# Filler matmuls placed behind the last scans' steps, and half of the attention's output projection moved into them

## The chip, the cores and the metric

The kernel runs on one core of one Trainium2 chip. The metric is device microseconds of one execution, of which the median over the runs is given. TensorE is called PE in the profile, VectorE DVE, ScalarE ACT, GpSimd POOL; SP is the engine that only issues DMAs here.

## The reference

One step of a decoder layer is computed for 1024 prompt tokens and for 8 samples of one token each, 1032 tokens in all, with a model width of 1024, all in float32:

```
h  = RMSNorm(x) * (1 + scale1) + shift1
z  = h @ w_in            # DeltaNet q|k|v, its gate, beta, decay; attention q, k, v; two branch gates ga, gb
y_a = GatedRMSNorm(GatedDeltaRule(conv4(q,k,v))) @ w_gdn_out      # 8 heads of 128
y_b = SlidingWindowSinkAttention(q, k, v) @ w_swa_out             # 16 query heads of 64, 4 kv heads, window 128
x  = x + gate1 * ((sigmoid(ga) * y_a + sigmoid(gb) * y_b) @ w_o)
h2 = RMSNorm(x) * (1 + scale2) + shift2
x  = x + gate2 * ((silu(dwconv3(h2 @ w_ffn_gate)) * (h2 @ w_ffn_up)) @ w_ffn_down)
y  = RMSNorm(x)
```

The prompt's gated delta rule runs in chunks from a zero state: per chunk a triangular inverse, and a recurrence over the chunks that carries a 128x128 state. The samples take one step of the same rule from states that are inputs (8 heads x 8 samples x 128x128), and give the new states back.

## The kernel before

**A product.** Every float32 product of the large projections is three matmuls on split operands: `mm3` (L168 to L170) multiplies high by high, high by low and low by high. An operand is split on ACT (L126, the high part) and DVE (L127, the rest). The split activations `h` (tiles b1h and b1l) stay resident in three parts of 384, 384 and 264 tokens (`PARTS`). A weight column of 128 outputs is one 512 KB load (L132), one split, and then, for each part, 8 blocks of 128 inputs with 3 matmuls each.

**The order.** The code is written as generators. `weave` runs several side by side, each with a priority and an increment, `later` runs a piece at a lower priority, and the scheduler of the framework then orders each engine's instructions from the priorities and its own estimate of the durations. What comes out is a fixed list for each engine, and each engine works its list from top to bottom: a matmul whose operand is late holds up all that stand behind it on PE. DMAs are issued from SP's list, a few from POOL's.

**The stages** that matter here, with their place in the profiled span:

- *Attention* (to 430 us): four groups of four query heads, each over 8 blocks of 128 tokens (`attention_block`): scores (L561, L562), transposes of the exponentials (L178), products with the values (L598, L600). Query and key projections lie between the blocks; none is left for the last ones.
- *Eight DeltaNet heads* (430 to 1182 us). For head h `weave` runs the triangular inverse (`unit_inverse`, L959 to L995, which goes through DRAM between its steps: `ud`, `MR`, `T`), the projections of head h+2, the gate projection of head h (`delta_gate`), the preparation of head h+1 (`delta_prepare`), and the scan (`delta_scan`). The scan has 8 chunks; a chunk is a chain of three steps on PE, each waiting for DVE or ACT: `rc<-S,K` (L870), `rc<-y,W` (L873), `rc<-s,kd` (L877), with two products for the output beside them (L880, L881).
- *Filler.* `gates()` is a generator of 16 tiles of work (8 for each branch gate): a column of `w_in`, 3 parts, 72 matmuls each, then tanh on ACT, a scaling on POOL and a store to DRAM (sgb, sga). `pieces(n)` pulls n x 8 of its steps. Each head pulls one tile at priority 10000, head 7 pulls the other eight within its `head_projections`.
- `turn_rows` in head 6 turns the input `x` in 9 chunks (load L771, 8 transposes, store L777) for later use; `last_rows` in head 7 gives back the last rows before the convolution (transposes of `zl`, copies L1027 to one of two `th` buffers, stores).
- *Branches* (1182 us on, `branches`). All of the attention's output `ob` is loaded and split in three parts (b2h, b2l), then y_b is computed: 8 columns of `w_swa_out` x 3 parts; the result times the gate is kept in SBUF (tiles t0 to t2, L1220). `sample_delta`, the samples' rule, is a generator that is stepped between these products: the loads of the states (b1h, b1l), small matmuls (L1084), 8 POOL products (L1124), 64 updates on DVE (L1126), 8 stores. Then y_a with `w_gdn_out`, then `w_o` and the second half, which the change leaves as it is.

## Time and profile before

| what | value |
|---|---|
| median of 3 runs | 2211.08 us (2209.51 to 2211.73) |
| profiled execution, its own time | 2216.06 us |
| span of the profiled execution | 2214.3 us |
| mean granted TensorE clock | 0.970 |
| PE busy / DVE / ACT / POOL | 96% / 60% / 36% / 14% of the span |

PE is busy nearly all of the time, so the table alone shows little. The stretches in which it isn't, and those in which the clock granted to it falls below full, are short and are found with busy times by stage. In the rows, "idle before, releaser" is time in which the engine had nothing to run, and what ended it.

### The profile page before, as it was taken

How to read it: one execution, taken by the hardware profiler on the slowest of the kernel's cores; microseconds unless marked ns; L12 is line 12 of the kernel's file. 1: busy time of each engine (PE TensorE's matmuls, PEld its weight loads, DVE VectorE, ACT ScalarE, POOL GpSimd, SP SyncE). 2: the span in 40 equal slices, each digit the busy share in tenths (PEclk: the TensorE clock that was granted, in tenths of full speed). 3: DMA queues.
4: the chain of work that ended last, by engine and by line, in shares of the span. 5: the costliest groups of instructions: out<-in, count | busy, mean ns of one | idle time of the engine just before them, and what ended most of it. 6: DMA issues, size and time to landing. Idle time of an engine off the chain costs nothing.

```text
span 2214.3 us, 41267 instructions
## 1 busy us (share of the span) xinstructions
PE 2123.2 (96%) x16573; PEld 1995.0 (90%) x16573; DVE 1335.3 (60%) x2892; ACT 801.2 (36%) x2037; POOL 303.3 (14%) x395
## 2 busy tenths in 40 slices
PE   7998999899899999999978999999999999999998
PEld 3695788699899999999968899999999999999998
DVE  4556667574474664755423565468776776866565
ACT  3445445433333334234332032344343433421102
POOL 2000000022122121121110200002332332100000
PEclk8998999799999999999988999999999999999999
DMA  9411333232232231232753663612323222253202
GB/s 340 140 40 39 115 117 106 82 79 49 73 83 69 53 91 52 65 89 73 199 140 107 206 187 99 184 61 68 108 70 96 68 94 70 96 215 129 88 3 78
DMA packets 271346, 228.16 MB, mean 103 GB/s; under 512 B 57566, under 2 KB 237697, under 8 KB 271138
## 3 DMA queue, kind: packets, MB, share of 16 engines
q1 hardware_dynamic: 269826, 221.23, 32.5%
q10 hardware_dynamic: 1152, 3.70, 0.4%
q8 instruction: 130, 2.13, 0.4%
q14 instruction: 62, 0.51, 0.1%
q0 software_dynamic: 176, 0.59, 0.1%
HBM read 175.51 MB, written 52.35 MB: 103 GB/s over the span
## 4 chain that ended last, share of the span: by engine, by line
PE 84%; DVE 6%; DMA 5%; ACT 2%; issue 1%; SPq 1%; POOL 0%; DVEq 0%; POOLq 0%; ACTq 0%
PE mm L168 19%; PE mm L169 18%; PE mm L170 18%; PE wv L168 2%; PE wv L169 2%; PE wv L170 2%; PE wy L170 2%; PE wy L168 2%; PE wy L169 2%; PE pv L600 1%; PE mm L252 1%; PE pv L598 1%; PE pt L178 1%; PE tp L178 1%; PE sc L561 1%
## 5 line engine op out<-in xcount | busy, mean ns | idle before, releaser
L168 PE MATMUL mm<-b1h,wh 128*128 128x384 f32 (+1 forms) x1440 | 476.0, 332 | 9.6 <-DVE kx L496 4.5
L170 PE MATMUL mm<-b1h,wl 128*128 128x384 f32 (+1 forms) x1440 | 469.2, 327 | 3.9 <-DVE wl L127 3.9
L169 PE MATMUL mm<-b1l,wh 128*128 128x384 f32 (+1 forms) x1440 | 468.8, 326 | 0.1
L168 PEld LDWEIGHTS mm<-b1h,wh 128*128 128x128 f32 x1440 | 274.3, 191 | 22.1 <-issue 6.3
L169 PEld LDWEIGHTS mm<-b1l,wh 128*128 128x128 f32 x1440 | 274.6, 191 | 8.6 <-issue 7.0
L170 PEld LDWEIGHTS mm<-b1h,wl 128*128 128x128 f32 x1440 | 274.0, 190 | 6.6 <-DVE wl L127 4.7
L126 ACT ACTIVATE wh<-raw 128x1024 fp32r<-128x1024 f32 x77 | 80.7, 1048 | 156.4 <-PE mm L169 103.0
L168 PE MATMUL mm<-b2h,wh 128*128 128x384 f32 (+1 forms) x384 | 123.9, 324 | 1.6 <-DVE t L1220 1.0
L168 PE MATMUL mm<-pk,w 128*128 128x260 f32 (+1 forms) x440 | 124.4, 283 | 0.9 <-ACT pk L126 0.6
L169 PE MATMUL mm<-pk,w 128*128 128x260 f32 (+1 forms) x440 | 124.2, 282 | 0.8 <-DVE pk L127 0.8
L169 PE MATMUL mm<-b2l,wh 128*128 128x384 f32 (+1 forms) x384 | 123.5, 322 | 1.2 <-DVE b2l L127 1.2
L170 PE MATMUL mm<-pk,w 128*128 128x260 f32 (+1 forms) x440 | 124.2, 282 | 0.0
L170 PE MATMUL mm<-b2h,wl 128*128 128x384 f32 (+1 forms) x384 | 122.7, 321 | 0.0
L127 DVE TENSOR_TENSOR wl<-raw,wh 128x1024 fp32r<-128x1024 f32 x76 | 93.7, 1233 | 45.6 <-ACT wh L126 44.7
L170 PE MATMUL mm<-bmh,pk 128*128 128x256 f32 (+1 forms) x380 | 108.6, 286 | 0.8 <-DVE pk L127 0.8
L168 PE MATMUL mm<-bmh,pk 128*128 128x260 f32 (+1 forms) x380 | 108.7, 286 | 0.0
L1342 DVE SCALAR_TENSOR_TENSOR x<-mm,mT,x 128x256 f32<-128x256 f32 (+2 forms) x133 | 63.4, 481 | 72.7 <-PE mm L170 70.3
L169 PE MATMUL mm<-bml,pk 128*128 128x260 f32 (+1 forms) x353 | 100.6, 285 | 0.0
L170 PE MATMUL mm<-bmh,w 128*128 128x260 f32 (+1 forms) x320 | 91.7, 287 | 0.0
L168 PE MATMUL mm<-bmh,w 128*128 128x260 f32 (+1 forms) x320 | 91.6, 286 | 0.0
L127 DVE TENSOR_TENSOR w<-ws,w 128x512 fp32r<-128x512 f32 x88 | 60.2, 685 | 41.6 <-ACT w L126 41.6
L168 PEld LDWEIGHTS mm<-pk,w 128*128 128x128 f32 x440 | 82.7, 188 | 1.5 <-ACT pk L126 0.8
(578 smaller groups left out, 5727.8 us busy)
## 6 DMA issues: line engine op xcount, KB each, us to landing
raw<-in_w_in_dram SPq DMA_DIRECT2D x60, 512.0 KB
bml<-act SPq DMA_DIRECT2D x22, 516.0 KB
raw<-in_w_ffn_gate_dram SPq DMA_DIRECT2D x22, 512.0 KB
raw<-in_w_ffn_up_dram SPq DMA_DIRECT2D x22, 512.0 KB
raw<-in_w_ffn_down_dram SPq DMA_DIRECT2D x22, 512.0 KB
qst<-in_w_mod_dram SPq DMA_DIRECT2D x16, 512.0 KB
raw<-in_w_mod_dram SPq DMA_DIRECT2D x16, 512.0 KB
act<-fa SPq DMA_DIRECT2D x22, 260.0 KB
```

The source lines that it names most:

```text
L126: self.nc.scalar.activation(hi, x, AF.Copy)
L127: (eng or self.nc.vector).tensor_tensor(lo, x, hi.bitcast(F32), op=ALU.subtract)
L168: mm(ps, whi, xhi, start=first, stop=False, **kw)
L169: mm(ps, whi, xlo, start=False, stop=False, **kw)
L170: mm(ps, wlo, xhi, start=False, stop=last, **kw)
L178: self.nc.tensor.transpose(out, in_, self.ident[:p, :p])
L252: nc.tensor.matmul(ps[32 * j:32 * j + 32], self.cT[:, k0 + j, :], ws[j // 2][:, j % 2, :], start=k0 == 0, stop=k0 > 0)
L561: nc.tensor.matmul(sc[:, r, 256 - w:256], q, KH[:, lo:lo + w], start=True, stop=False)
L598: nc.tensor.matmul(out, V[:, n, ch], pc[:, r::2, :], start=True, stop=n == 0)
L600: nc.tensor.matmul(out, V[:, n - 1, ch], pp[:, r::2, :], start=False, stop=True)
L1342: nc.vector.scalar_tensor_tensor(x[:, :np_], ps[:, :np_], self.mT[:, m + j, 8:9], x[:, :np_], op0=ALU.mult, op1=ALU.add)
```

## The change

It changes when work is done, and where some of it keeps its results; the matmuls of the products stay the same in number and, by and large, in size.

1. **Gates in attention.** `gates()` starts in attention: 24 steps each (one gate tile) after the half-groups 5 and 6 of 8.
2. **Filler in the heads.** Heads 0 to 5 pull 5 x 8 steps each, at the same priority 10000, so ten tiles; head 6 pulls the last four in `head_projections`.
3. **A second filler, `first_branch`,** follows the gates in the same generator, and head 7 pulls it. It is the y_b projection for tokens 0 to 511: 8 columns x 8 steps x 3 matmuls of 512 columns. Its operands are loaded into tiles of the heads that are free by then (high in K2, Q2, K0, Q0; low in kd, A, vn, v0). The results times the gate go to DRAM (`ubd`) through two `gt` tiles, stored from POOL's queue. Every second step also steps the samples' rule.
4. **`spaced`.** In heads 6 and 7 two filler steps at a time are tied behind one scan step's matmul in PE's order.
5. **The samples' DMAs** go from SP's queue to POOL's: state loads, `dlr`, broadcasts, new states, `oa`.
6. **Branches** have the parts 512, 260 and 260 (`BRANCH`). The y_b columns for the last two load and split `w_swa_out` a second time, from ACT's queue. y_b of these goes to `ubd` too, and comes back for y_a as the low tiles of the mix.
7. `last_rows` goes from priority 1000 to 200 with an increment of 20, the scan's first output transposes go from chunk 3 to chunk 5, and `delta_gate` gets a stream of its own.

The core of the diff:

```diff
+            for _ in range((0, 0, 0, 0, 0, 24, 24, 0)[2 * g + n0 // 4]):
+                self.later(lambda: next(self.filler), 120)
...
+        self.filler, self.fill_where, self.gt = chain(self.gates(), self.first_branch()), [self.where], (pool, "mrows")
...
+                with self.spaced():
+                    self.mm3(ps, whi[:, k, :], wlo[:, k, :], xh[:, k, :], xl[:, k, :], k == 0, k == KC - 1)
...
+    def spaced(self):
+        if not self.steps:
+            return nullcontext()
+        self.at += 1
+        i = min(self.at // 2, len(self.steps))
+        return self.tc.issue_after(self.steps[i - 1]) if i else nullcontext()
...
+    def first_branch(self):
+        X = self.load_half(self.ob)
+        self.samples = self.sample_delta()
+        self.ubd = self.t(self.dr, [8, P, NT], "ubd")
+        w = load(0)
+        for j in range(8):
+            s = self.t(self.gt[0], [P, 512], self.gt[1], bufs=2)
+            self.sgb_loads.append(nc.sync.dma_start(s, self.sgb[j][:, 0:512]))
+            def out(t, ps):
+                nc.vector.tensor_tensor(s, ps, s, op=ALU.mult)
+                nc.gpsimd.dma_start(self.ubd[j][:, 0:512], s)
+            for i, step in enumerate(self.project_steps(w, {0: X}, out, (0,), self.fill_psum, BRANCH)):
+                if i == 0 and j < 7:
+                    ahead = load(j + 1)
+                if i % 2:
+                    next(self.samples, None)
+                yield
...
-            nc.sync.dma_start(S0[h], I["state_gdn_S"][0][:, h].rearrange("b k v -> k b v"))
+            nc.gpsimd.dma_start(S0[h], I["state_gdn_S"][0][:, h].rearrange("b k v -> k b v"))
...
-                               (self.pieces(3), 10000, 100)]
+                               (self.head_projections(pa, pool, h), 600, 100)]
+                    if h + 2 < H:
+                        streams.append((self.pieces(5), 10000, 100))
...
-                        streams.append((self.last_rows(pa), 1000, 0))
+                        streams.insert(0, (self.last_rows(pa), 200, 20))
```

How the rows of the engines move is seen at three places; `x4` after a row is a count of equal rows.

**PE, last blocks of attention.** `sc` are scores, `pt` transposes, `pv` products with the values. Before, the blocks follow each other with nothing between:

```order
L561 MATMUL sc_3591<-kh_2531,qst_3101 128x256
L562 MATMUL sc_3591<-kl_2533,qst_3101 128x256
L178 MATMUL pt_3527<-ident,E_3494 128x128 x4
L561 MATMUL sc_3598<-kh_2531,qst_3196 128x256
L562 MATMUL sc_3598<-kl_2533,qst_3196 128x256
```

Now a gate tile (`mm_652`, 24 matmuls of its third part here) stands between the transposes of one block and the products that follow:

```order
L586 MATMUL sc_677_4031<-kh_427_2531,qst_558_3292 128x256
L587 MATMUL sc_677_4031<-kl_429_2533,qst_558_3292 128x256
L201 MATMUL pt_671_4008<-ident_75,E_665_3975 128x128 x4
L191 MATMUL mm_652_3897<-b1h2_14_152,wh_646_3835 128x264
L192 MATMUL mm_652_3897<-b1l2_15_153,wh_646_3835 128x264
L193 MATMUL mm_652_3897<-b1h2_14_152,wl_647_3836 128x264
```

Two gate tiles have moved here; behind the second, 20 rows of the last two or three blocks still stand bare.

**PE, head 7's scan.** Before, some 45 rows (from `zl` on) hold the scan's steps alone, with a few transposes among the first:

```order
L870 MATMUL rc_12146<-S_12143,K_9579 128x128
L880 MATMUL o_12130<-S_12143,Q_9580 128x128
L873 MATMUL rc_12149<-y_12145,W_4141 128x128
L877 MATMUL rc_12153<-s_12151,kd_10766 128x128
L881 MATMUL o_12130<-s_12151,A_10818 128x128
L870 MATMUL rc_12160<-S_12157,K_9579 128x128
```

Now the scan's first four chunks have transposes of `z` and `zl` among them but hardly a product:

```order
L900 MATMUL rc_12238<-S_12235,K_1650_10225 128x128
L910 MATMUL o_12213<-S_12235,Q_1651_10226 128x128
L903 MATMUL rc_12241<-y_12237,W_4332 128x128
L907 MATMUL rc_12245<-s_12243,kd_11606 128x128
L911 MATMUL o_12213<-s_12243,A_11658 128x128
L900 MATMUL rc_12252<-S_12249,K_1650_10225 128x128
L910 MATMUL o_12213<-S_12249,Q_1651_10226 128x128
L903 MATMUL rc_12255<-y_12251,W_4332 128x128
L201 MATMUL mm_11820<-ident,z_11818 128x128 x4
L201 MATMUL mm_11826<-ident,z_11818 128x128 x4
```

and the later chunks have 19 or 20 products between two steps (`first_branch`, here its third column, around one step):

```order
L193 MATMUL mm_2052_12746<-K0_2005_12356,wl_2049_12629 128x512
L191 MATMUL mm_2052_12746<-Q0_2006_12357,wh_2048_12628 128x512
L903 MATMUL rc_1997_12327<-y_1995_12323,W_711_4332 128x128
L192 MATMUL mm_2052_12746<-v0_2010_12361,wh_2048_12628 128x512
L193 MATMUL mm_2052_12746<-Q0_2006_12357,wl_2049_12629 128x512
```

Of the four gate tiles of head 6, two stand solid ahead of head 7's inverse; between them and the scan's fifth chunk PE's list has the inverse, 72 transposes of `z`, 24 products and the transposes of `zl`.

**SP, the loads of `z`.** Before, the chunks of `z` are loaded and stored among the first stores of a head's inverse (`ud`) and the gates' stores:

```order
L132 DMA raw_12522<-in_w_swa_out_dram 128x8x128
L771 DMA z_10903<-in_x_prompt_dram 128x1024
L777 DMA xT_10870<-K_10871 128x8x128
L918 DMA ud_11008<-G_10759 32x8x32 x2
L771 DMA z_10918<-in_x_prompt_dram 128x1024
L777 DMA xT_10870<-Q_10872 128x8x128
```

Now the third chunk and all later ones stand behind the stores of the last gate tile (`sga`) and behind the gate loads of `first_branch` (`gt<-sgb`), which need the same two `gt` tiles:

```order
L1230 DMA sga_3101<-gt_11537 128x384
L1230 DMA sga_3101<-gt_11566 128x384
L1250 DMA gt_12381<-sgb_3100 128x512
L794 DMA z_11743<-in_x_prompt_dram 128x1024
L800 DMA xT_11710<-K_1866_11711 128x8x128
L1230 DMA sga_3101<-gt_11595 128x264
```

So `z` is turned later than before relative to the gates: most of it after the last of them, during head 7's inverse and first chunks.

More of the change, by code (lines that the diff above doesn't have):

```diff
@@ L60, in carver, with __init__, __getitem__ @@
     return small
+class Pairs:
+    def __init__(self, tiles):
+        self.tiles = [t.rearrange("p n i -> p (n i)").rearrange("p (a n) -> p a n", a=2) for t in tiles]
+    def __getitem__(self, key):
+        _, k, cols = key
+        return self.tiles[k // 2][:, k % 2, cols]
 class Step:
@@ L76, in __init__ @@
         self.lo_engine = None
-        self.filler, self.ahead, self.fill_psum = iter(()), False, self.pmf
+        self.filler, self.fill_psum = iter(()), self.pmf
+        self.steps, self.at = [], 0
+        self.n_gate, self.w_queue = 0, None
     def pool(self, name, bufs, space=None, ctx=None, side=None):
@@ L859, in delta_scan, with step @@
         S = None
+        self.steps, self.at = [], 0
+        def step(ins):
+            if h + 2 >= H:
+                self.steps.append(ins.ins)
         so = self.t(pool, [P, NCH], "so", bufs=2)
@@ L1208, in branches, with load_half @@
+    def load_half(self, src):
+        his, los = self.rooms[:4], self.rooms[4:]
+        for i in range(4):
+            hi, lo = (x.rearrange("p n i -> p (n i)") for x in (his[i], los[i]))
+            raw = lo.bitcast(F32)
+            self.nc.sync.dma_start(raw.rearrange("p (k n) -> p k n", k=2),
+                                   src[2 * i:2 * i + 2, :, 0:512].rearrange("k p n -> p k n"))
+            self.split(hi, lo, raw)
+        return Pairs(his), Pairs(los)
     def branches(self, pool, pool2):
@@ L1209, in branches @@
         nc, I = self.nc, self.I
-        ob = [self.load_part(pool2, self.ob, t) for t in range(3)]
-        ub = [self.t(pool, [P, KC, n], f"t{t}", bufs=1) for t, (_, n) in enumerate(PARTS)]
-        self.fill_where, self.gt, self.ahead, self.fill_psum = self.where, (pool, "sgx"), True, None
+        ob = {t: self.load_part(pool2, self.ob, t) for t in (1, 2)}
         for _ in self.filler:
             pass
-        samples = self.sample_delta()
-        next(samples)
-        gate = lambda src, j, t: self.gate_part(pool, src[j][:, PARTS[t][0]:PARTS[t][0] + PARTS[t][1]], t)
+        gate = lambda src, j, t: self.gate_part(pool, src[j], t)
```

136 lines of the change are left out of this document (77 added, 59 removed).

## The prediction

> **What bounds the kernel now.** First the page: busy times, the granted clock in 40 slices, the chain that ended last, and the two groups of splits that feed PE.
>
> ```profile
> PE 2123.2 (96%) x16573; PEld 1995.0 (90%) x16573; DVE 1335.3 (60%) x2892; ACT 801.2 (36%) x2037; POOL 303.3 (14%) x395
> PEclk8998999799999999999988999999999999999999
> PE 84%; DVE 6%; DMA 5%; ACT 2%; issue 1%; SPq 1%; POOL 0%; DVEq 0%; POOLq 0%; ACTq 0%
> L126 ACT ACTIVATE wh<-raw 128x1024 fp32r<-128x1024 f32 x77 | 80.7, 1048 | 156.4 <-PE mm L169 103.0
> L127 DVE TENSOR_TENSOR wl<-raw,wh 128x1024 fp32r<-128x1024 f32 x76 | 93.7, 1233 | 45.6 <-ACT wh L126 44.7
> ```
>
> TensorE is the bound: 96% busy, 84% of the chain, so DVE and ACT matter only where PE waits for them. The change keeps PE's products; it can win only what PE loses today, by idling or by running at a lower granted clock. The clock falls in slice 8 (388 to 443 us) and slices 21 and 22 (1107 to 1218 us). Second view, busy times by stage (after the engines: clock, DMA share, GB/s):
>
> ```profile
> 380.00:400.00 20.00, 18.35 (x97) 13.61 (x97) 12.77 (x57) 10.91 (x45) 0.00 (x0) 0.70 0.13 52
> 400.00:420.00 20.00, 13.62 (x70) 8.43 (x68) 14.13 (x46) 11.27 (x44) 1.12 (x3) 0.84 0.10 30
> 420.00:440.00 20.00, 17.61 (x87) 14.67 (x86) 6.02 (x12) 7.92 (x32) 2.37 (x3) 0.69 0.62 185
> ...
> 1060.00:1080.00 20.00, 18.32 (x132) 17.55 (x131) 7.13 (x15) 9.38 (x24) 7.61 (x12) 1.00 0.87 238
> 1080.00:1100.00 20.00, 18.42 (x138) 18.07 (x137) 11.46 (x38) 7.06 (x15) 1.56 (x4) 1.00 0.98 271
> ...
> 1120.00:1140.00 20.00, 18.49 (x151) 17.05 (x150) 6.90 (x17) 6.05 (x14) 3.64 (x6) 1.00 0.72 190
> 1140.00:1160.00 20.00, 10.71 (x45) 7.79 (x43) 3.77 (x10) 4.55 (x15) 1.01 (x1) 0.65 0.66 185
> 1160.00:1180.00 20.00, 13.31 (x44) 10.95 (x44) 7.69 (x16) 10.57 (x23) 3.63 (x4) 0.50 0.50 175
> ...
> 1240.00:1260.00 20.00, 16.54 (x93) 16.02 (x92) 18.19 (x48) 1.56 (x2) 7.07 (x5) 0.91 0.74 210
> 1260.00:1280.00 20.00, 18.64 (x114) 18.01 (x113) 10.69 (x31) 1.06 (x1) 6.13 (x3) 1.00 0.94 285
> ```
>
> I count a stage's loss as idle time plus busy time x (1 - clock):
>
> - **A, end of attention, 380 to 440:** idle 1.65 + 6.38 + 2.39 = 10.4; clock 18.35 x 0.30 + 13.62 x 0.16 + 17.61 x 0.31 = 13.1. Together 23.5 us.
> - **E, head 7, 1060 to 1180:** idle 1.68 + 1.58 + 1.51 + 9.29 + 6.69 = 20.8; clock 10.71 x 0.35 + 13.31 x 0.50 = 10.4. Together 31 us.
> - **F, samples' rule beside y_b, 1240 to 1280:** idle 3.46 + 1.36, clock 1.5. Together 6.3 us.
>
> All three give 61 us, the ceiling of what this change can win. The heads between are nearly full, with one exception:
>
> ```profile
> 560.00:600.00 40.00, 36.22 (x396) 34.26 (x395) 16.40 (x47) 11.34 (x31) 6.09 (x9) 0.91 0.21 59
> ...
> 880.00:920.00 40.00, 40.00 (x274) 39.96 (x273) 28.84 (x69) 11.43 (x26) 9.78 (x14) 1.00 0.35 83
> ```
>
> **The change part by part: the end of attention.** What is one gate tile worth as filler? The spacing of the matmuls, here of 384 columns, not their overlapping durations:
>
> ```profile
> 885.90 0.34 PE L168 MATMUL mm<-b1h,wh 128*128 128x384 f32 x1
> 886.07 0.33 PE L169 MATMUL mm<-b1l,wh 128*128 128x384 f32 x1
> 886.25 0.34 PE L170 MATMUL mm<-b1h,wl 128*128 128x384 f32 x1
> ...
> PE sc L561 <- DVE E L567: 3.4, 3, 2.3
> PE pt L178 <- ACT E L582: 2.6, 2, 1.9
> ```
>
> A matmul takes 0.173 us, so the 264-column part about 0.173 x 264 / 384 = 0.119 (estimate), and a tile 24 x (0.173 + 0.173 + 0.119) = 11.2 us. Two tiles, 22 us, lie down in stage A where PE today waits for exponentials (the last two rows, waits from 380 to 432). 22 us of filler can cover 10.4 us of idling and keep the clock up. But the order shows it in three lumps, and 20 of the roughly 100 formerly bare rows stand bare behind it. I leave 20/100 of 23.5 = 5 us for these, and 5 more for lumps that come ahead of a wait rather than in it: **A = -13** (bounds -8 and -18). ACT's tanh of the gates are six more operations among the exponentials; with ACT at 11 of 20 us, no cost.
>
> A rule speaks here. The Trainium skill ("TensorE: Matmul & The Clock Gate", Part 1: The HAM clock gate) has the clock at half or full, and falling only after an idle window of about 3.4 us. The trace bears the levels out (0.50 in one row), but not the gap: the longest wait of stage A is 2.3 us and the clock still fell to 0.69. By the rule the few bare blocks left would run at full speed, some 3 us better than my sum; I go by the trace.
>
> **Heads 0 to 6: +1.** The gates leave these heads sooner or later by a tile; rows of 40.00 of 40 can't improve. At the seams of heads 5 and 6 the new order has two short bare stretches, which I put at 1 us (0 to 4). The hole at 560 to 600 is a wait for a gate tile's split, which stands in both orders: no gain.
>
> **Head 7: -7.** Today's loss has these causes:
>
> ```profile
> PE rc L178 <- DVE vn L899: 7.4, 2, 4.0
> PE mm L178 <- ACT th L1027: 5.3, 2, 4.2
> ...
> L178 PE MATMUL mm<-ident,z x72: 200/272/299, 1059.3 to 1097.7; 128*128 128x128 f32 x64, 8*128 8x8 f32 x8
> ...
> 1141.69 4.93 DMA out_dram<-th
> 1156.94 0.80 PE rc L877 x2
> 1158.18 0.79 PE rc L870 x2
> 1159.42 0.81 PE rc L873 x2
> 1168.97 6.14 DMA b2l<-ob
> ```
>
> The scan runs bare at 1.24 us a step (three rows above), with the clock at 0.50; then y_b waits 6.14 for its operands. Afterwards the second half of the scan is covered: 12 steps x 1.24 = 15 us at most; the load of `ob` comes earlier (its halves stand in SP's list ahead of the last gates), 6 us. `vn`'s two waits come with chunk 4 and the end: one is covered now. That is -15 - 6 - 3.7 = -25 if nothing new appears. What appears: `z`'s nine chunks took 38.4 us (1059.3 to 1097.7), 4.3 each, with products between all of them. Now chunks 3 to 9, 7 x 4.3 = 30 us, stand behind the last gate, in a stretch of PE's list that has little of its own: 56 transposes and 24 products at 0.17 (13 us if the transposes count as much), 160-odd small inverse products and a dozen scan steps, some 5 more (estimate). The inverse needs its DRAM round trips anyway, about 20 us of these 30 as last time. So 30 - 18 = 12 us of new idling, and a lower clock for the rest, at 0.65 as at 1140: 18 x 0.35 = 6. **Head 7 = -25 + 12 + 6 = -7**, bounds -20 (the turn runs as fast as its DMAs alone, and the clock stays) and +4 (the stretch is paced by the `th` round trip of 4.93 too: two buffers, six copies, two more waits).
>
> **Samples' rule and y_b: +5.** This work moves into a stretch where DVE and POOL already had their hands full:
>
> ```profile
> L1126 DVE SCALAR_TENSOR_TENSOR b1h<-b1h,egb,b1l 128x128 f32<-128x128 f32 x40 | 14.7, 436 | 5.1 <-POOL b1l L1124 5.1
> L1220 DVE TENSOR_TENSOR t<-mm,sgx 128x384 f32<-128x384 f32 x16 | 8.8, 552 | 30.3 <-PE mm L170 30.3
> L1126 DVE SCALAR_TENSOR_TENSOR b1l<-b1l,egb,b1l 128x128 f32<-128x128 f32 x24 | 8.3, 414 | 3.6 <-POOL b1l L1124 3.6
> ...
> L1124 POOL TENSOR_TENSOR b1l<-b1l,kq 128x1024 f32<-128x1024 f32 x8 | 15.7, 1964 | 77.6 <-DMA b1l<-dlr 69.5 <-DVE t L1220 8.0
> ```
>
> The updates are 14.7 + 8.3 = 23 us of DVE, as before. New are eight more splits of `w_swa_out`: 8 x 1.233 = 9.9 us of DVE, 8 x 1.048 = 8.4 of ACT. For y_b's later parts PE has 8 x 48 matmuls x 0.118 (260 columns, by the spacing above) = 45 us, and the samples' small products; DVE has there about 23 + 8 x 1.233 + 16 x 0.43 + 5 for a half of `oa` = 45. It is level, no longer slack. DMA: `ubd` written and read again (8.4 MB) and 4 MB of weights are new; from the fifth chunk to the end of y_b I count weights 8, states in and out 8, broadcasts 4, gates 4, `ubd` 4, operands 4 = 32 MB in 44 + 45 + 17 = 106 us of PE work, 300 GB/s. The fastest rows above moved 271 and 285. At 285 it takes 112 us: +6. At worst nothing of it is hidden (+10); at best the state loads come early enough (0). **F = +5.** The page "DMA: Bandwidth & Descriptors" of the Trainium skill (Issuing engines are not separate DMA queues) says that transfers issued on several engines end on the same 16 DMA engines; no row here separates the queues enough to show it. By it the move to POOL's queue buys no bandwidth, and my count in bytes stands as it is; if POOL's queue did add bandwidth, F would be 0.
>
> The parts 512, 260, 260 instead of 384, 384, 264 cost nothing: the same 1032 columns at the same spacing per column. y_a reads `ubd` back on a stretch of 88 us with 15 MB: nothing.
>
> **Sum:** -13 + 1 - 7 + 5 = **-14 us** against the profiled execution's own 2216.06 (span 2214.3 and 1.8 around it): 2202. The median of the runs shown, 2211.08, is 5.0 below that execution, so I forecast **2197 us**.
>
> **The rivals.**
>
> - *All holes close:* A -18, head 7 -20, F 0, heads 0: -38 + 3 for seams, **2176**. For it speaks that the order puts filler behind every late step, against it the bare inverse and the position of `z`.
> - *Only attention gains:* head 7's losses are just moved to the inverse and `z` (0 to +4), F +6: -13 + 1 + 2 + 6 = -4, **2207**. For it speaks the DMA share of 0.98 while `z` was turned.
> - *POOL's queue holds PE up, and it ends slower.* `first_branch` has two `gt` tiles; a column's store stands in POOL's list among the samples' eight products of 1.964 us and their broadcasts. Store late, gate load late, product late, PSUM late: PE waits. POOL spent 69.5 us waiting for the broadcasts. If the samples' chain POOL, DVE, store runs in series instead of beside, it takes 15.7 + 45 = 61 us against PE's 45: +16, and three or four column stores that each wait out a transfer (4.93 us, as `th` did) less one column of slack are some +10: F is +26 instead of +5, the sum +7, **2218**. It decides as soon as F exceeds 14 + 4.4 + 5 = 23 us, that is when a column takes 8.5 instead of 5.5 us over all eight. Against it: the PSUM tiles, three in turn, and the alternating weights.
> - *The change doesn't do what it says:* the ties of `spaced` come so late that filler runs ahead of the steps and the scan ends bare as before. Then only A counts against F: **2204**; the order speaks against it.
>
> **How the numbers follow.** Forecast 0.45 (its own range 2187 to 2207), all holes close 0.17, only attention 0.17, POOL's queue 0.17, no effect in head 7 0.04. A measurement of this kernel tells 0.2%, 4.4 us, from no change. Faster: 0.45 + 0.17 + 0.04 and a little of the attention case, less the tail of the forecast: 0.68. Same: 0.14. Slower: 0.18. The range of 2172 to 2221 leaves out the best of the second case and the worst of the fourth.
>
> **What would show it.** A: rows from 380 to 440 with the clock near 0.9 and under 4 us of idling. Head 7: `z`'s transposes over 30 us or more, with the clock below 1.00 there; full rows after the scan's fifth chunk; no wait for b2l of 6 us. F: waits of PE for a split or for `gt` in the y_b rows, DMA share above 0.9 over 100 us. The forecast is wrong if `z` is turned early and covered (then the second case), or if POOL's waits for broadcasts stand ahead of stores (the fourth).

## The result: 0.93% slower, and the profile after

The changed kernel takes 2232.76 us (median of 4 runs, 2229.66 to 2236.01) against 2211.4 us for the kernel before in the same measurements: ratio 1.0093, 95% interval [1.0069, 1.0116], or some 21 us lost. Forecast were 14 us won, with a range that ended at 2221. The profiled execution took 2231.3 us, with a span of 2229.6 us and a mean granted clock of 0.969. First the page of the changed kernel, the same lines as before:

```profile
PE 2120.6 (95%) x16573; PEld 1982.0 (89%) x16573; DVE 1345.3 (60%) x2892; ACT 806.4 (36%) x2029; POOL 336.9 (15%) x453
PEclk8999999899999999999989999899999999999999
PE 83%; DVE 5%; DMA 5%; ACT 3%; issue 2%; SPq 1%; POOL 0%; DVEq 0%; POOLq 0%; ACTq 0%
L141 DVE TENSOR_TENSOR wl<-raw,wh 128x1024 fp32r<-128x1024 f32 x84 | 103.8, 1236 | 72.3 <-ACT wh L140 70.7
```

PE has the same 16573 matmuls and the same work; the eight more splits are there (84 for 76). The clock is better in slice 8 (8 for 7), and there is a new dip in slice 26 (1394 to 1449 us). Busy times by stage of the changed kernel:

```profile
380.00:400.00 20.00, 19.62 (x134) 17.28 (x132) 15.35 (x40) 10.36 (x37) 0.98 (x1) 0.99 0.16 53
400.00:420.00 20.00, 18.80 (x99) 17.13 (x99) 9.18 (x35) 6.43 (x26) 0.51 (x1) 0.76 0.12 39
420.00:440.00 20.00, 12.45 (x72) 8.36 (x72) 10.17 (x26) 9.33 (x33) 1.68 (x2) 0.84 0.15 43
...
940.00:960.00 20.00, 18.73 (x246) 17.47 (x245) 5.03 (x11) 9.71 (x32) 3.24 (x5) 0.90 0.19 57
960.00:980.00 20.00, 19.53 (x136) 18.73 (x136) 11.95 (x32) 7.24 (x32) 5.24 (x8) 0.93 0.30 87
...
1020.00:1060.00 40.00, 37.75 (x383) 35.23 (x381) 18.91 (x49) 18.59 (x73) 8.68 (x13) 0.91 0.27 74
...
1100.00:1120.00 20.00, 16.32 (x277) 14.08 (x275) 2.96 (x5) 8.49 (x19) 6.68 (x7) 0.91 0.92 269
1120.00:1140.00 20.00, 8.03 (x50) 6.88 (x48) 0.89 (x3) 4.79 (x10) 0.00 (x0) 0.58 0.86 268
1140.00:1160.00 20.00, 15.58 (x107) 13.09 (x108) 6.02 (x14) 9.28 (x25) 1.03 (x1) 1.00 0.25 65
1160.00:1180.00 20.00, 19.39 (x105) 16.29 (x104) 10.09 (x24) 4.95 (x8) 4.70 (x7) 1.00 0.49 140
...
1200.00:1220.00 20.00, 16.29 (x60) 12.51 (x60) 10.68 (x23) 5.80 (x9) 7.74 (x10) 0.83 0.63 193
...
1240.00:1260.00 20.00, 11.65 (x68) 10.88 (x67) 11.63 (x23) 5.90 (x6) 6.84 (x9) 0.82 0.99 357
1260.00:1280.00 20.00, 17.73 (x132) 17.31 (x133) 14.01 (x27) 3.18 (x3) 9.60 (x11) 0.92 0.67 198
```

Read them against the rows of before: the last blocks of attention are now full until 400, and from there on the clock falls again (0.76 and 0.84); the scan of head 7 is full from 1160 to its end, where it had run at half clock; and two deep holes are new, 1120 to 1140 (PE busy 8.03 of 20) and 1240 to 1260 (11.65 of 20, with the DMA engines at 0.99). The rows from 940 to 980 and from 1020 to 1060 were fuller in before:

```profile
940.00:960.00 20.00, 19.61 (x177) 18.18 (x176) 5.18 (x11) 9.95 (x34) 3.49 (x5) 1.00 0.19 58
960.00:980.00 20.00, 19.59 (x143) 19.07 (x142) 12.74 (x31) 7.94 (x30) 3.92 (x5) 1.00 0.36 109
...
1020.00:1060.00 40.00, 39.55 (x464) 37.21 (x463) 16.32 (x39) 18.43 (x66) 5.63 (x7) 1.00 0.20 67
```

Where the two gate tiles of attention lie is seen in ACT's tanh, which ends each of a tile's three parts. The last part of the first tile and the first part of the second, and then the row of before that holds the place of the first tile (its other two parts end at 313.5 and 323.3):

```profile
329.47 0.39 ACT L1228 ACTIVATE mrows<-mm 128x264 f32<-128x264 f32 x1 [0.92 <-PE mm L193]
413.94 0.49 ACT L1228 ACTIVATE mrows<-mm 128x384 f32<-128x384 f32 x1 [0.48 <-PE mm L193]
```

```profile
280.00:330.00 50.00, 50.00 (x327) 40.81 (x325) 30.13 (x84) 24.66 (x83) 0.20 (x2) 1.00 0.33 109
```

So one of the two stands where PE was full already, and only the second among the bare blocks.

To compare kernels whose stages shift, I add up, in steps of 5 us, idle time and busy time x (1 - clock), between points of the program: from 330 us to the last product of attention plus 3 us, then to 107 us ahead of head 7's last scan step `rc<-y,W`, 14 us behind it, 6 us ahead of the first product with `w_o`, and 56 us on. "End" is the end of attention, "heads" are 0 to 6 with the start of 7; "y" is the rest of y_b and y_a. Losses in us of one profiled execution each; ratios against runs of the kernel before on the same chip:

| kernel | ratio, interval | end | heads | head 7 | y | w_o |
|---|---|---|---|---|---|---|
| before | 1 | 22.1 | 18.3 | 31.5 | 6.3 | 7.6 |
| **changed** | 1.0093 [1.0069, 1.0116] | 16.2 | 26.7 | 24.9 | 23.9 | 14.8 |
| before + two gates in attention | 1.0009 [0.9993, 1.0025] | 16.0 | 18.1 | 43.4 | 6.0 | 5.6 |
| changed, no gates in attention | 1.0082 [1.0062, 1.0102] | 23.0 | 23.4 | 16.6 | 37.8 | 11.6 |
| **base**: changed, states on SP | 1.0026 [1.0012, 1.0041] | 16.2 | 24.6 | 21.5 | 25.1 | 12.2 |
| changed, samples later | 1.0099 [1.0077, 1.0120] | 17.4 | 23.6 | 26.8 | 33.7 | 8.5 |
| base, 3 x 8 filler steps | 1.0071 [1.0043, 1.0099] | 15.4 | 42.5 | 14.7 | 28.1 | 11.2 |
| base, two weights | 1.0007 [0.9989, 1.0025] | 16.3 | 22.4 | 22.1 | 19.4 | 10.8 |
| base, no updates | 0.9987 [0.9969, 1.0004] | 16.1 | 22.3 | 30.2 | 6.2 | 12.0 |
| base, ubd on SP | 1.0022 [1.0009, 1.0036] | 16.1 | 22.1 | 19.5 | 24.8 | 10.8 |
| base, loads without updates | 1.0013 [1.0001, 1.0026] | 16.1 | 25.5 | 30.5 | 14.0 | 11.9 |
| base, POOL without DVE | 1.0041 [1.0025, 1.0057] | 16.0 | 25.4 | 30.6 | 19.5 | 11.7 |
| base, no ties | 1.0032 [1.0014, 1.0049] | 15.8 | 22.2 | 20.5 | 26.3 | 11.7 |
| base, old streams, 3 x 8 | 1.0089 [1.0065, 1.0113] | 16.0 | 36.6 | 12.7 | 33.9 | 10.2 |
| base, 6 x 8 | 1.0034 [1.0017, 1.0051] | 16.0 | 15.3 | 27.5 | 26.2 | 11.9 |
| base, transposes at chunk 3 | 1.0110 [1.0083, 1.0137] | 15.5 | 37.1 | 25.4 | 22.4 | 11.9 |
| **before + transposes at chunk 5** | 0.9954 [0.9938, 0.9969] | 22.2 | 18.5 | 24.2 | 6.8 | 3.5 |
| the same + two gates | 0.9971 [0.9957, 0.9985] | 15.7 | 16.5 | 33.7 | 6.8 | 9.6 |

How far one such reading can be trusted is seen ahead of 330 us. From 180 to 230 the rows of PE stand in the same order in both kernels, and yet before runs there at a lower clock than the changed kernel:

```profile
180.00:230.00 50.00, 44.05 (x257) 30.41 (x259) 32.75 (x109) 26.61 (x106) 0.00 (x0) 0.86 0.24 83
180.00:230.00 50.00, 43.86 (x276) 29.14 (x275) 34.53 (x116) 28.75 (x114) 0.00 (x0) 0.97 0.27 87
```

Counted in steps of 5 us, this stretch loses 12.6 to 12.9 us in five of the eighteen profiles (before, 3 x 8, no ties, transposes at chunk 3, the last row) and 7.3 to 8.4 in the others, some of either kind with the gates in attention and some without. It lies well ahead of the gates and goes with no part of the change, so the table leaves it out. In the other columns, too, a difference under 5 us between two rows means little. The end of attention is steadier: 22.1 to 23.0 in the three kernels without the gates there, 15.4 to 17.4 in the fifteen with them.

The changed kernel against before: end of attention -5.9, heads +8.4, head 7 -6.6, y +17.6, w_o +7.2; the start and the second half together +2. The sum is 22.7, and the medians differ by 21. (The spans differ by 15.3 only, mostly because the profiled execution of before lost 5.2 us more between 130 and 330.) Where the holes come from is read in the waits of the changed kernel's PE from 1040 to 1400:

```profile
PE tp L1027 <- ACT UZ L1024: 11.1, 1, 11.1
PE mm L191 <- ACT wh L140: 6.1, 3, 3.7
PE mm L191 <- DVE gt L1253: 5.2, 3, 4.2
PE mm L1385 <- ACT w L140: 5.0, 1, 5.0
PE mm L201 <- DMA z<-in_x_prompt_dram: 2.4, 2, 1.8
PE mm L193 <- DVE wl L141: 2.2, 2, 1.7
```

and in its chain of work, where it goes through the two holes:

```profile
1110.92 18.53 DMA xT<-K
1129.58 0.44 issue
1130.02 0.59 ACT K L799
1130.64 0.59 ACT UZ L1024
1131.27 1.96 PE tp L1027 x16
...
1232.65 12.31 DMA raw<-in_w_swa_out_dram
1245.04 1.07 ACT wh L140
1246.13 1.24 DVE wl L141
```

**The first hole**, 11 us in head 7's inverse: the store of a turned chunk of `x` took 18.53 us. ACT's next copy of `z` needs that buffer and waits; the inverse's copy `UZ` stands behind it in ACT's list; PE stands before `UZ`. What shared the DMA engines with the store were six of the eight loads of the samples' states, which POOL issued back to back:

```profile
1110.75 2.91 POOL L1074 DMA_DIRECT2D b1l<-in_state_gdn_S_dram  x3 [7.23 <-PE mm L193]
1113.65 2.63 POOL L1074 DMA_DIRECT2D b1h<-in_state_gdn_S_dram  x3
```

**The second hole**: a column of `w_swa_out` took 12.31 us to land. Behind it stand ACT's and DVE's splits, of the operands of y_a too, and one of `first_branch`'s products. SP's waits from 1200 to 1262 show a store chain as well; a gate load waited for a `gt` tile until its column had been stored:

```profile
SPq L1250 <- DMA ubd<-gt: 26.7, 4, 10.7
```

The DMA engines moved 357 GB/s in that hole. This is no record: before moved as much in an early row, with all its transfers issued from SP.

```profile
20.00:40.00 20.00, 17.13 (x80) 8.35 (x78) 6.67 (x12) 4.60 (x8) 0.00 (x0) 0.76 1.05 362
```

### The profile page after: what moved, and what is told of

Read it like the earlier page. It is cut to its first block, busy times and chain, and to the rows that moved or that the text cites. A ratio compares the mean times of both kernels' runs of the same rounds, so it can differ in the third digit from the quotient of the medians.

```text
span 2229.6 us, 41358 instructions
## 1 busy us (share of the span) xinstructions
PE 2120.6 (95%) x16573; PEld 1982.0 (89%) x16573; DVE 1345.3 (60%) x2892; ACT 806.4 (36%) x2029; POOL 336.9 (15%) x453
## 4 chain that ended last, share of the span: by engine, by line
PE 83%; DVE 5%; DMA 5%; ACT 3%; issue 2%; SPq 1%; POOL 0%; DVEq 0%; POOLq 0%; ACTq 0%
PE mm L191 19%; PE mm L192 18%; PE mm L193 18%; PE wv L192 3%; PE wv L193 3%; PE wv L191 3%; PE wy L193 2%; PE wy L191 2%; PE wy L192 2%; PE mm L275 1%; PE pt L201 1%; PE pv L625 1%; PE pv L623 1%; DMA xT<-K 1%; PE tp L201 1%
## 5 line engine op out<-in xcount | busy, mean ns | idle before, releaser
L140 ACT ACTIVATE wh<-raw 128x1024 fp32r<-128x1024 f32 x85 | 89.0, 1048 | 178.7 <-PE mm L192 120.5
L141 DVE TENSOR_TENSOR wl<-raw,wh 128x1024 fp32r<-128x1024 f32 x84 | 103.8, 1236 | 72.3 <-ACT wh L140 70.7
L192 PEld LDWEIGHTS mm<-pk,w 128*128 128x128 f32 x440 | 82.8, 188 | 1.0 <-DVE pk L141 1.0
L191 PEld LDWEIGHTS mm<-pk,w 128*128 128x128 f32 x440 | 82.8, 188 | 1.0 <-ACT pk L140 0.8
L191 PE MATMUL mm<-b2h,wh 128*128 128x260 f32 x256 | 74.7, 292 | 9.3 <-DVE gt L1253 5.0
L193 PEld LDWEIGHTS mm<-pk,w 128*128 128x128 f32 x440 | 83.0, 189 | 0.0
```

Of the source, the lines that this page charges most:

```text
L140: self.nc.scalar.activation(hi, x, AF.Copy)
L141: (eng or self.nc.vector).tensor_tensor(lo, x, hi.bitcast(F32), op=ALU.subtract)
L191: mm(ps, whi, xhi, start=first, stop=False, **kw)
L192: mm(ps, whi, xlo, start=False, stop=False, **kw)
L193: mm(ps, wlo, xhi, start=False, stop=last, **kw)
```

## The experiments

Three theories to tell apart. **Stock:** filler is a fixed stock, and moving a tile only moves the hole. **Bytes:** the stretches behind head 7's inverse carry more DMA traffic than they have time for, and single loads come late. **Queue order:** the column stores are late because they stand behind the samples' rows in POOL's list (the prediction's case that POOL's queue holds PE up).

**Gates in attention alone**, on the kernel before.

```diff
...
+            for _ in range((0, 0, 0, 0, 0, 24, 24, 0)[2 * g + n0 // 4]):
+                self.later(lambda: next(self.filler), 120)
...
```

> The kernel before with the first part of the change alone: two gate tiles in attention. If the parts add, attention loses 11 us less (23 to 12, as in the changed kernel) and nothing else moves: ratio to before 0.995, about 2200 us. The rival: the filler is a stock of 16 tiles, and head 7, which had nine of them, now has seven; then the 22 us of cover go missing there and its loss of 31 us grows by 10 to 20: ratio 1.000 to 1.004, 2211 to 2220 us, with rows of low clock from 1080 us on.

Measured: 1.0009. The end of attention lost 6 us less, head 7 12 us more. (The 11 us for attention in this expectation, in the next and in that of the last pair count the stretch from 180 to 230 too.) The rows of this run, head 7's scan without cover from 1120 on:

```profile
1120.00:1140.00 20.00, 15.25 (x150) 13.57 (x144) 6.85 (x17) 8.16 (x25) 2.18 (x3) 0.66 0.59 154
1140.00:1160.00 20.00, 12.04 (x55) 9.30 (x53) 4.67 (x14) 4.92 (x16) 1.04 (x2) 0.63 0.52 150
1160.00:1180.00 20.00, 13.31 (x45) 10.88 (x45) 7.44 (x16) 10.57 (x23) 3.63 (x4) 0.51 0.50 172
```

Three rows of low clock where before had two. The rival of the expectation holds: filler is a stock, and the hole that is filled gains less than the place it is taken from loses.

**The changed kernel without them.**

```diff
-            for _ in range((0, 0, 0, 0, 0, 24, 24, 0)[2 * g + n0 // 4]):
+            for _ in range((0, 0, 0, 0, 0, 0, 0, 0)[2 * g + n0 // 4]):
```

> The changed kernel without the two gate tiles in attention; they fall to head 7, ahead of first_branch. If the parts add: attention's 11 us come back, 2244 us. If the filler is a stock whose place only decides which hole is filled, the two tiles fill head 7's inverse and the turn of z (20 us of idling there now): 2230 to 2236 us, with the 11 us wait of the inverse gone.

Measured: 1.0082, not told apart from 1.0093. Head 7 falls from 24.9 to 16.6, and the 11 us wait is gone; the end of attention rises from 16.2 to 23.0; y rises too, from 23.9 to 37.8. The stock again, and a first sign that y takes back what head 7 gains.

**States on SP.**

```diff
-            nc.gpsimd.dma_start(S0[h], I["state_gdn_S"][0][:, h].rearrange("b k v -> k b v"))
+            nc.sync.dma_start(S0[h], I["state_gdn_S"][0][:, h].rearrange("b k v -> k b v"))
```

> The changed kernel with the eight loads of the samples' states back in SP's queue, as before. Theory of contention in head 7: these 4 MB, issued from POOL at 1110 us, make the store of turned z take 18.5 us, and ACT and the inverse stand behind it for 11 us; behind z in SP's queue they don't: 8 to 11 us less, 2222 to 2225 us, and the 18.5 us store near 5. Rival, total bytes: the same 4 MB then fall on the y_b stretch, which is full, and the time is given back there: 2230 to 2240 us.

Measured: 2217.88 us, 1.0026: most of the loss is gone with one word. ACT's waits from 1095 to 1150, of the changed kernel and then of this one:

```profile
ACT K L799 <- DMA xT<-K: 12.6, 1, 12.6
```

```profile
ACT K L799 <- DMA xT<-K: 5.2, 2, 3.6
ACT Q L799 <- DMA xT<-Q: 3.8, 1, 3.8
```

The first state loads start at 1110.8 in both. From SP's list they go out one after another between the loads and stores of `z`, the sixth some 12 us after the first instead of 5, and the longest wait for a store is 3.8 instead of 12.6 us. The wait of PE that stood behind that store was 11.1 us and is now

```profile
PE tp L1027 <- ACT UZ L1024: 1.3, 1, 1.3
```

So it is shown that the burst of loads held up the store, and PE behind it. Where all of the 15 us lie is not: the two profiles show 8 of them (this one's execution, 2223.36 us, lies 5.5 us above its median), and head 7 only 3.4, since other waits for the turn of `z` grow. y doesn't fall: the bytes are as many. This kernel is the base of most that follow.

**Samples later:** `first_branch` doesn't step the samples' rule.

```diff
-                if i % 2:
-                    next(self.samples, None)
```

> The changed kernel, but the samples' rule is not stepped from first_branch; all of it is stepped from the two later parts of y_b. If the stores of first_branch wait because they stand behind the samples' rows in POOL's queue, head 7's columns run free and 5 us are won there; if bytes and DVE time in the y_b stretch are what counts, the samples' 17 MB and 23 us of updates now fall into some 50 us and the time grows by 10 us or more: 2243 us or above. I expect the second.

Measured: 1.0099, the same as the changed kernel. The loss in y rises by 10 us, w_o's falls by 6; neither of the two expectations is met clearly.

**3 x 8 filler steps** in heads 0 to 5 (base).

```diff
-                        streams.append((self.pieces(5), 10000, 100))
+                        streams.append((self.pieces(3), 10000, 100))
```

> The changed kernel with the states' loads in SP's queue (the one that came out at 1.0026 of before), and 3 x 8 filler steps instead of 5 x 8 in heads 0 to 5, so that four more gate tiles are left for heads 6 and 7. If the 8 us that heads 0 to 6 lose more than before come from the doubled filler taking ACT and DVE from the scan, they go: 1.000 or below. If the place of the filler only decides which hole is filled, heads 0 to 5 lose nothing or gain little, head 7's inverse is covered (10 us of idling there) and columns of first_branch slide out behind the scan: 0.998 to 1.003.

Measured: 1.0071. Neither alternative: the heads lost 18 us more, head 7 only 7 less.

**Old streams** with 3 x 8 steps (base): `delta_gate` again as the first part of `head_projections`.

```diff
+        yield from self.delta_gate(pa, pool, h)
...
-                               (self.delta_gate(pa, pool, h), 500, 1),
-                               (self.delta_scan(pool, psum, h, prep), 100, 1),
-                               (self.head_projections(pa, pool, h), 600, 100)]
+                               (self.head_projections(pa, pool, h), 500, 100),
+                               (self.delta_scan(pool, psum, h, prep), 100, 1)]
...
-                        streams.append((self.pieces(5), 10000, 100))
+                        streams.append((self.pieces(3), 10000, 100))
```

> The base with the heads' streams as they were before the change: the gate projection first in head_projections at priority 500 with an increment of 100, and 3 x 8 filler steps. With 3 x 8 steps alone the heads had lost 42 us instead of 25 (ratio 1.0071). If that came from taking the gate projection out of the spaced stream, the heads go back to the 18 us of before and the four gate tiles kept serve head 7 (15 us instead of 21): 12 us less than the base, ratio 0.996 to 0.999, better than both kernels. If it came from something else in the changed streams, 1.002 to 1.008.

Measured: 1.0089; the heads lose 36.6, some 6 less than with 3 x 8 steps alone. The streams aren't the main reason.

**6 x 8 filler steps** (base), two gate tiles in head 6 instead of four.

```diff
-            for _ in range(8 if h + 1 == H else 4):
+            for _ in range(8 if h + 1 == H else 2):
...
-                        streams.append((self.pieces(5), 10000, 100))
+                        streams.append((self.pieces(6), 10000, 100))
```

> The base (states' loads in SP's queue) with 6 x 8 filler steps in heads 0 to 5 and two gate tiles instead of four in head 6. With 3 x 8 steps the heads had lost 42 and 37 us instead of 25. If the heads' loss is missing filler at their seams, it falls below 20 us, and head 7, with 22 us of filler less ahead of its inverse, loses as much more (30 instead of 21): 1.002 to 1.005. If it comes from elsewhere, the heads stay at 23 to 26 us and the ratio is 1.004 or above.

Measured: 1.0034. The heads fall to 15.3 and head 7 rises to 27.5, as the first alternative said (below 20, about 30). With 42.5 for 3, 24.6 for 5 and 15.3 for 6, more filler closes the holes at the heads' seams; the total hardly moves. But filler alone isn't the whole account: the kernel before gives its heads 3 x 8 steps as well and loses only 18.3 there. What else in the change opens the holes that its extra filler then closes was not found.

**Transposes at chunk 3** (base): the move of the scan's output transposes undone.

```diff
-            if n in (5, NCH - 1):
+            if n in (3, NCH - 1):
```

> The base with the transposes of the scan's first half back at chunk 3. Before the change PE waited 7.4 us for vn with them there in head 7. If the move to chunk 5 is worth that wait, head 7 loses 3 to 4 us more, and the heads before it up to 1 each: 1.004 to 1.006. If the filler covers it anyway, within 0.0015 of 1.0026; if the move is what costs the heads their 8 us, 0.999 to 1.001.

Measured: 1.0110. Some 18 us for one number, more than any expectation; the heads lose 12 us more and head 7 loses 4 us more. PE's waits for vn from 440 to 1400, of this kernel and then of the base:

```profile
PE rc L201 <- DVE vn L929: 4.4, 3, 3.8
```

```profile
PE o L910 <- DVE vn L929: 0.4, 1, 0.4
PE rc L201 <- DVE vn L929: 0.3, 1, 0.3
```

They are 4 us longer and don't make up 18; where the rest comes from is not settled. So, of the parts that were undone, the move to chunk 5 was worth most, and I took it alone:

**Transposes at chunk 5 alone**, on the kernel before.

```diff
+            if n in (5, NCH - 1):
+                c0 = 4 if n == NCH - 1 else 0
                 tp = self.t(psum, [P, 4, P], "rc", bufs=2)
                 for c in range(4):
-                    self.transpose(tp[:, c, :], on[:, c, :])
+                    self.transpose(tp[:, c, :], vn[:, c0 + c, :])
```

> The kernel before with one part of the change alone: the transposes of the scan's first half at chunk 5 instead of 3. In the changed kernel putting them back cost 0.84% (18 us), 12 of it in heads 0 to 6. If the move is as good without the rest, before gains what it waits there: its 7.4 us for vn in head 7 halve, and the holes at 540 to 580 and 860 (some 9 us) shrink: 0.995 to 0.998. If 18 us were a matter of the order that the scheduler happened to find for the changed kernel, 0.999 to 1.001.

Measured: 2202.36 us, 0.9954 [0.9938, 0.9969]: **faster than both kernels**, some 10 us below before. Head 7 loses 24.2 instead of 31.5, and the wait for vn is one of 4.0 instead of two of 7.4 (1050 to 1400):

```profile
PE rc L178 <- DVE vn L899: 4.0, 1, 4.0
```

The heads, whose holes were to shrink, lose as much as before (18.5 and 18.3).

**The same with the two gates in attention** (the edits of both kernels).

> The same with the two gate tiles in attention as well (alone they had come out at 1.0009: 11 us won in attention, 12 lost in head 7). If filler is a stock, the ratio is that of the late transposes alone, within 0.0015; if the late transposes leave head 7 in need of less filler, the two add up to 0.003 below it.

Measured: 0.9971, the intervals overlap; head 7 rises from 24.2 to 33.7. The stock a third time.

**No ties** (base): `spaced` gives no ties at all.

```diff
-        if not self.steps:
+        if True:
             return nullcontext()
```

> The same kernel as the base (states' loads in SP's queue) without the ties of filler steps behind the scan's steps. If the ties are what covers the scan of head 7, head 7 loses 10 us more: ratio 1.007 or above. If the scheduler places the filler as well by the priorities alone, within 0.002 of 1.0026.

Measured: 1.0032, within 0.002 of the base; head 7 loses 20.5 against 21.5. The ties, by which the change is named, do nothing that can be measured here.

Now the stretch of y. **Two weights** (base):

```diff
-            w = self.load_w(I["w_swa_out"][0][:, j * P:(j + 1) * P], where=sides[j % 2])
+            if j < 2:
+                oa["w", j] = self.load_w(I["w_swa_out"][0][:, j * P:(j + 1) * P], where=sides[j % 2])
+            w = oa["w", j % 2]
```

> The same kernel (states' loads in SP's queue), but the two later parts of y_b load and split only the first two columns of w_swa_out and use them for all eight, so that y_b's last 520 tokens are computed with the wrong columns: 3 MB, 6 splits on ACT and DVE less. If the second load of the weights is what the y_b stretch waits for (PE waited there 7 us for wh and wl, and a load took 12 us), its loss of 23 us falls to 12 to 16 and the ratio to 0.996 to 0.999. If the store chain of first_branch or the samples' rows set the pace, the ratio stays within 0.002 of 1.0026.

Measured: 1.0007 with an interval that overlaps the base's; the loss in y falls from 25.1 to 19.4, short of the 12 to 16 expected. The second load of the weights is a part of it, not all.

**ubd on SP** (base):

```diff
-                nc.gpsimd.dma_start(self.ubd[j][:, 0:512], s)
+                nc.sync.dma_start(self.ubd[j][:, 0:512], s)
...
-            nc.gpsimd.dma_start(self.ubd[j][:, lo:lo + n], u)
+            nc.sync.dma_start(self.ubd[j][:, lo:lo + n], u)
```

> The same kernel, with the stores of y_b times the gate (ubd) in SP's queue instead of POOL's. If these stores are late because they stand behind the samples' rows in POOL's queue (POOL waited 12.5 us for a DVE row with one of them behind), the waits of PE for gt (5.5 us) go and the ratio is 0.999 to 1.001. But SP's queue then waits for DVE's products ahead of weight and operand loads; if that costs as much, the ratio stays at 1.002 to 1.005. I expect the second.

Measured: 1.0022, y 24.8, as expected. PE's waits for `gt` fall from 5.5 to 4.0 us only. But at these stores SP's list now waits 46 us for DVE (1180 to 1300), the price that the expectation named, so this run by itself can't tell a wrong theory from a trade. The next run speaks against the theory. SP's wait for these stores, from 1180 to 1300, of the changed kernel and then of the next run (no updates), in which the samples' broadcasts and products are gone from POOL's list:

```profile
SPq L1250 <- DMA ubd<-gt: 29.4, 5, 10.7
```

```profile
SPq L1243 <- DMA ubd<-gt: 39.8, 4, 19.5
```

Without these rows the wait is longer, not shorter, and y loses 6.2 us there, not 23.9.

**No updates; loads without updates; POOL without DVE** (base): three steps of putting the second half of the samples' rule back.

```diff
...
-            nc.gpsimd.dma_start(d, dlr[h].unsqueeze(0).broadcast_to([P, NS, P]))
-            nc.gpsimd.tensor_tensor(d, d, bc(kq[:, h, :, 0], 2, P), op=ALU.mult)
-            for b in range(NS):
-                nc.vector.scalar_tensor_tensor(S0[h][:, b, :], S0[h][:, b, :], self.egb[:, b, 0, h:h + 1], d[:, b, :],
-                                               op0=ALU.mult, op1=ALU.add)
```

(all of these lines out; then the first one in again; then the first two.)

> The same kernel, but the samples' states are written back as they were loaded: the eight broadcasts (4 MB), the eight POOL products and the 64 updates on DVE are left out. If POOL's and DVE's work for the samples sets the pace of y_b (16 and 27 us, ahead of column stores and splits), its loss falls from 23 to below 12: ratio 0.996 to 0.998. If bytes do, 4 of 31 MB fall away, some 14 us of transfers of which half shows: 0.999 to 1.001.

> The changed kernel with the states' loads in SP's queue (1.0026 of before), the broadcasts loaded as they are, but POOL's eight products and DVE's 64 updates left out, so that the samples' states are written back as they came. Without the broadcasts as well the ratio had been 0.9987 and the loss of the stretch from the end of the scan to w_o 6 instead of 25 us. If the bytes made the difference, they are back now and the loss is 18 us or more, the ratio 1.001 to 1.003. If POOL's and DVE's work did, the loss stays below 10 us and the ratio at 0.998 to 1.000. I expect the second.

> The same kernel with broadcasts and POOL's products, and only DVE's 64 updates left out (27 us of DVE). If it is DVE's list, in which splits and column products stand behind runs of 8 to 24 updates, the loss behind the scan stays below 10 us (ratio 0.998 to 1.000); if it is POOL's list, in which the column stores stand behind the products and their waits, it goes back to 18 us or more (1.001 to 1.003).

Measured: 0.9987, 1.0013, 1.0041, against 1.0026 with all of it. Without the updates y loses 6.2 us, as much as before the change. Its rows for the same work:

```profile
1220.00:1240.00 20.00, 19.60 (x111) 16.81 (x110) 5.80 (x7) 3.39 (x4) 3.55 (x6) 1.00 0.77 253
1240.00:1260.00 20.00, 20.00 (x168) 20.00 (x169) 12.10 (x16) 7.94 (x8) 5.58 (x10) 1.00 0.92 283
1260.00:1280.00 20.00, 20.00 (x169) 19.96 (x168) 6.56 (x11) 3.38 (x4) 5.08 (x9) 1.00 0.84 254
```

PE is full with the DMA engines at 0.92. In all three the order of head 7 came out otherwise than in the base (its loss is 30 us, with waits for `z` of 9 to 11 us), so I compare head 7 and y together: 36.4, then 44.5 with the 4 MB of broadcasts, 50.1 with POOL's products, 46.6 with DVE's updates too. By these sums, of one profile each, the broadcasts carry 8 us and POOL's products 6; by the medians it is 6 and 6. DVE's 27 us of updates carry nothing. The expectation of the second run, the engines and not the bytes, fell, but y's 14.0 us lie between its two alternatives, and the broadcasts bring back their rows in POOL's list along with their bytes. Of the two times 0.9987 and 1.0013 the intervals just overlap; the step from 1.0013 to 1.0041 has intervals that touch at 1.0025.

## Why the prediction was wrong

- **What bounds the kernel, the ceiling:** right. PE's work stayed the same, 2120.6 against 2123.2 us busy, and the whole difference is idling and clock.
- **A = -13: mis-sized, and its step "two tiles lie down in stage A" failed.** The end of attention gained 5.9 us, outside the bounds of -8 and -18. Only one of the two tiles stands in that stage; the other lies at some 303 to 329 us, where PE had nothing to lose. The bare rows at 420 to 440 are where they were expected, but the signs that the prediction set for A failed: the rows from 380 to 440 have 9.1 us of idling, not under 4, and the clock is 0.99, 0.76 and 0.84. The second tile itself began at a low clock: its matmuls of 384 columns follow each other every 0.32 us from 406 on, and every 0.17 us from 410. No wait of PE from 380 to 420 is longer than 1.2 us, so the trace's side of the argument on the clock holds.
- **Head 7 = -7: right in size**, -6.6, in part by luck. The scan's second half is covered, and the turn of `z` behind the last gate took 48.7 us (1097.6 to 1146.3) and opened the hole that was forecast. But the worst 11 us of that hole come from a store held up by the state loads, which was not in the working: the state loads' move to POOL's queue was costed at nothing by counting bytes alone. The run with the state loads on SP is 15 of the 21 us faster.
- **The step that failed most: F = +5**, mis-sized. y lost 17.6 us more than before. The 32 MB were counted rightly (30.6 MB from 1180 to 1300), but dividing them by the fastest rate of the rows shown, 285 GB/s, and taking the excess, 6 us, is the wrong sum. That rate was no ceiling: before itself moved 362 GB/s from 20 to 40 us, and the changed kernel 357 from 1240 to 1260. At 357 GB/s the 32 MB take 90 us (estimate), less than the 106 us of PE's work, and y lost 17.6 us all the same. What the traces show there is that single loads come late, 12.31 us for a column of weights, with the splits and PE's waits for `wh`, `wl` and `gt` behind them. The runs without broadcasts and with two weights show that 4 and 3 MB less bring 8 and 6 us, by one profile each.
- **Heads = +1**, measured +8.4: "bounds 0 to 4" was too narrow. The place was right, the seams of heads 5 and 6: the rows 940 to 980 and 1020 to 1060 lose 10.6 us, against 1.3 in before. More filler in the heads closes them, as 3, 5 and 6 x 8 steps show, and takes it from head 7.
- **w_o, costed at nothing**, measured +7.2. PE waits 5.0 us for the first split of `w_o`, whose load SP issues 5 us ahead of the first product, not 10 as before. The diff puts the pools of `branches` into the outer stack; that their release is what holds the load is argued, not tried.
- **The rivals.** The case of POOL's queue, the only one on the slower side, ended nearest (2218), and the chain that it named is there: 26.7 us of SP's waits for `ubd`. But in the run without updates, where the samples' rows are gone from POOL's list, the wait is longer and y loses only 6.2 us. So the case was right that this stretch is where the time goes, and the runs speak against the cause that it named, the stores' place in POOL's list. "All holes close" and "only attention gains" fail for one reason that the prediction left out: what fills one hole is missing in another. The sum added A's gain and took nothing off elsewhere, though it said itself that the tiles come out of the heads and head 7. Gates in attention alone win 6 us in their place and lose 12 in head 7.

What stays open: why the transposes at chunk 3 cost 18 us in the changed kernel when the waits for vn make up 4 of them; what costs the heads of the changed kernel some 20 us more than before when both give them 3 x 8 steps; where the rest of the 15 us of the state loads lies; and how much of y's loss is the samples' traffic beside the doubled weight loads, of which neither run alone reaches the size.

## What to carry to other kernels

Filler is a stock: before a tile is moved into a hole, name the place where it stood and read what that place loses without it; a sum that books only the gain is wrong by its own size or more. A stretch with DMA engines near full isn't priced by bytes over rate alone: ask which load comes late and what stands behind it in each engine's list; and which queue issues a burst decides whose transfer is late. In a change of many parts, undo each alone: here the move of four transposes, the least of the edits, is worth 10 us by itself, and the rest takes that back and 21 us more.

## What the runs showed of the hardware

- Six loads of 512 KB, issued within 5.5 us from POOL, stretched a store of 512 KB from SP to 18.53 us; the same loads issued from SP's list, between the stores, left none of ACT's waits for such a store above 3.8 us. The Trainium skill ("DMA: Bandwidth & Descriptors", Issuing engines are not separate DMA queues) says that transfers interleave on the same 16 DMA engines whichever engine starts them. The trace agrees: nothing was won in bandwidth (269 and 268 GB/s in the rows from 1100 to 1140, against 271 and 285 with the loads on SP), and the store shared the engines with the burst. What the choice of the queue changes is when the burst is let loose.
- DMA traffic reached 357 GB/s over 20 us at a share of 0.99 with SP, ACT and POOL issuing (1240 to 1260), and 362 in before with SP alone (20 to 40 us).
